# Bulk rows laid out by partition: one run of 126 rows per partition, stored without TensorE and PSUM

## Chip, cores, metric

One core of one Trainium2 chip. The metric is device time in microseconds (us) of one execution; the median of several executions is quoted, and a profiled execution gives the lines shown. A profile's span, from first to last instruction, is some 1.8 us shorter than the device time of the same run.

## The reference

```python
x = np.random.randn(64, 256, 8192).astype(np.float32)   # 536.87 MB
out = np.mean(x, axis=2)                                # 16,384 means, 64 KB
```

That is 16,384 rows of 8192 float32, 32 KiB each, read once.

## The kernel before

63 bulk loads bring 256 rows each (8 MiB) into one of three slots of SBUF: partition p gets two neighbouring rows, 64 KiB. VectorE sums both into `res`. The last 256 rows come in a cut-up tail, so that little is left to sum after the last byte. The results of the bulk lie with the row pair on partitions and the block number along the free axis; to store them in order, TensorE transposes `res`.

```python
NB = N // (P * R); LB = NB - 1                     # 64 blocks, 63 of them bulk; P = 128, R = 2
x_v = x_f.rearrange("(n p r) s -> n p r s", p=P, r=R)
out_bulk = o_f[0 : LB * P * R].rearrange("(n p r) -> n p r", p=P, r=R)
# ... (cut)
for n in range(LB):
    xt = slots[n % SLOTS]                          # SLOTS = 3
    ld = load(xt[:], x_v[n], load_sem[n % LOAD_SEMS])
    if n < LB - 1:
        loaded(n, dve_sum(res[:, :, n], xt[:]))
    else:                                          # last bulk block: half on ScalarE
        loaded(n, dve_sum(res[:, 0, n : n + 1], xt[:, 0, :]))
        loaded(n, act_sum(res[:, 1, n : n + 1], xt[:, 1, :]))
# ... (cut: the tail: head = 8192 columns of 128 rows, then 4096, 2048, ... 256, 256)
bulk = pool.tile([P, P, R], F32)
for r in range(R):
    ps = psum_pool.tile([P, P], F32, name=f"ps{r}")
    nc.tensor.transpose(out=ps[:LB, :], in_=res[:, r, :], identity=ident[:])
    nc.vector.tensor_scalar_mul(out=bulk[:LB, :, r], in0=ps[:LB, :], scalar1=inv)
nc.sync.dma_start(out=out_bulk, in_=bulk[:LB])     # 63 pieces of 1 KiB
# ... (cut: scaled sums and stores of the tail)
```

## Time and profile before

| | before |
|---|---|
| median of 3 runs | 1246.19 us (1246.14 to 1246.21) |
| span of the profiled run | 1244.9 us |
| VectorE busy | 1087.4 us, 87% |
| TensorE matmuls and weight loads | 0.9 + 0.4 us |
| DMA | 431 GB/s over the span |

### The profile page before, as it was taken

Reading aid. Unit: us, or ns where it says so; the run is one execution under the profiler, and the core shown is the slowest. Engines: PE = TensorE matmul, PEld = TensorE weight load, DVE = VectorE, ACT = ScalarE, POOL = GpSimd, SP = SyncE. Lnnn points to the kernel's source line nnn. Section 1 sums busy time; section 2 is a strip of 40 time slices with the busy share of each in tenths; the row PEclk is TensorE's granted clock in tenths of the full one; section 3 lists DMA queues with packets and bytes.
Section 4 is the critical chain, followed back from the end, with each engine's and each line's share of the span. In section 5 each row is a group of like instructions: output and inputs, shape, how many; then the busy total and the mean of one; then the engine's idle time right before and its main releaser. Section 6 shows DMA issues by size and latency. Waiting matters only on the chain.

```text
span 1244.9 us, 214 instructions
## 1 busy us (share of the span) xinstructions
PE 0.9 (0%) x2; PEld 0.4 (0%) x2; DVE 1087.4 (87%) x79; ACT 16.5 (1%) x13; POOL 0.7 (0%) x6
## 2 busy tenths in 40 slices
PE   0000000000000000000000000000000000000000
PEld 0000000000000000000000000000000000000000
DVE  3898988989889889898898988989889898898898
ACT  0000000000000000000000000000000000000004
POOL 0000000000000000000000000000000000000000
DMA  9999999999999999999999999999999999999998
GB/s 436 406 438 438 438 438 432 415 434 438 438 438 438 438 425 417 438 438 438 438 438 436 409 436 438 438 438 438 438 427 415 438 438 438 438 438 436 409 436 373
DMA packets 10169, 536.95 MB, mean 431 GB/s; under 512 B 1145, under 2 KB 1464, under 8 KB 1720
## 3 DMA queue, kind: packets, MB, share of 16 engines
q1 hardware_dynamic: 10168, 536.94, 99.8%
q14 instruction: 1, 0.01, 0.0%
HBM read 536.87 MB, written 0.07 MB: 431 GB/s over the span
## 4 chain that ended last, share of the span: by engine, by line
DMA 70%; DVE 29%; SPq 0%; issue 0%; DVEq 0%
DMA xt<-in_x_dram 70%; DVE res L92 29%; DVE fin_in L92 0%; SPq L82 0%; DVE fin_in L98 0%; DVE fin_t L109 0%; DVEq L98 0%
## 5 line engine op out<-in xcount | busy, mean ns | idle before, releaser
L92 DVE TENSOR_REDUCE res<-xt 128x2 f32<-128x16384 f32 (+1 forms) x63 | 1076.4, 17086 | 153.5 <-DMA xt<-in_x_dram 153.5
L95 ACT ACT_TABLE_LOAD x1 | 1.3, 1283 | 1181.5 <-DVE res L92 1181.5
L95 ACT ACTIVATE xt<-xt 128x8192 f32<-128x8192 f32 (+5 forms) x6 | 14.7, 2443 | 43.9 <-DMA xt<-in_x_dram 43.7
L92 DVE TENSOR_REDUCE fin_in<-xt 128x1 f32<-128x256 f32 (+3 forms) x5 | 5.0, 1004 | 0.3 <-DMA xt<-in_x_dram 0.2
L92 DVE TENSOR_REDUCE head<-xt 128x1 f32<-128x4096 f32 x1 | 4.4, 4420 | 0.2 <-DMA xt<-in_x_dram 0.2
L153 PE MATMUL ps<-ident,res 128*63 128x128 f32 x2 | 0.9, 458 | 1230.5 <-ACT xt L95 1229.5
L95 ACT ACTIVATION_READ_ACCUMULATOR xt<-xt 128x1 f32 x6 | 1.1, 186 | 0.0
L72 DVE MEMSET fin<- 128x32 f32 x2 | 0.1, 85 | 0.9 <-PEq L254 0.9
L154 DVE TENSOR_SCALAR bulk<-ps 63x128 f32<-63x128 f32 x2 | 0.6, 279 | 0.4 <-PE ps L153 0.4
L153 PEld LDWEIGHTS ps<-ident,res 128*63 128x63 f32 x2 | 0.4, 180 | 1230.8 <-issue 1229.4
L98 DVE TENSOR_SCALAR_CACHE_REDUCE fin_in<-fin_in 128x265 f32<-128x265 f32 x1 | 0.4, 431 | 0.2 <-DVE fin_in L92 0.2
L109 DVE STREAM_TRANSPOSE fin_t<-fin 128x32 f32<-128x32 f32 x2 | 0.4, 211 | 0.1
L60 POOL TENSOR_SCALAR_AFFINE_SELECT ident<-ident 128x128 f32<-128x128 f32 x1 | 0.3, 292 | 0.1
L98 DVE TENSOR_SCALAR_CACHE_REDUCE head<-head 128x2 f32<-128x2 f32 x1 | 0.2, 155 | 0.1
L59 POOL MEMSET ident<- 128x128 f32 x1 | 0.2, 204 | 0.4 <-POOLq L254 0.4
L254 POOL MEMSET const-bfloat16-1.0<- 128x1 bf16 x1 | 0.1, 101 | 0.0
L254 POOL MEMSET const-uint8-127<- 128x1 uint8 x1 | 0.1, 101 | 0.0
L254 POOL MEMSET const-float32-0.0<- 128x1 f32 x1 | 0.1, 98 | 0.2 <-issue 0.2
L254 POOL MEMSET const-float32-1.0<- 128x1 f32 x1 | 0.1, 98 | 0.0
L98 DVE DVE_READ_ACCUMULATOR head<-head 128x1 f32 x1 | 0.1, 83 | 0.0
L98 DVE DVE_READ_ACCUMULATOR fin_in<-fin_in 128x1 f32 x1 | 0.1, 83 | 0.0
## 6 DMA issues: line engine op xcount, KB each, us to landing
xt<-in_x_dram SPq DMA_DIRECT2D x1, 4096.0 KB, 31.1
xt<-in_x_dram SPq DMA_DIRECT2D x1, 2048.0 KB, 35.7
xt<-in_x_dram SPq DMA_DIRECT2D x1, 1024.0 KB, 37.7
xt<-in_x_dram SPq DMA_DIRECT2D x63, 40.8
xt<-in_x_dram SPq DMA_DIRECT2D x1, 512.0 KB, 38.5
xt<-in_x_dram SPq DMA_DIRECT2D x1, 256.0 KB, 38.7
xt<-in_x_dram SPq DMA_DIRECT2D x1, 128.0 KB, 38.6
fin_in<-in_x_dram SPq DMA_DIRECT2D x1, 128.0 KB, 38.4
```

The source lines that it names most:

```text
L59: nc.gpsimd.memset(ident[:], 0.0)
L60: nc.gpsimd.affine_select(out=ident[:], in_=ident[:], compare_op=mybir.AluOpType.not_equal, fill=1.0, base=0, pattern=[[-1, P]], channel_m ...
L72: nc.vector.memset(fin[r][:], 0.0)
L92: return untracked(nc.vector.tensor_reduce(out=dst, in_=src, axis=X, op=ADD))
L95: return untracked(nc.scalar.activation(out=src, in_=src, func=COPY, accum_out=dst))
L98: return nc.vector.tensor_scalar(out=src, in0=src, scalar1=inv, scalar2=None, op0=mybir.AluOpType.mult, op1=ADD, accum_out=dst,)
L109: nc.vector.transpose(out=fin_t[r][:], in_=fin[r][:])
L153: nc.tensor.transpose(out=ps[:LB, :], in_=res[:, r, :], identity=ident[:])
L154: nc.vector.tensor_scalar_mul(out=bulk[:LB, :, r], in0=ps[:LB, :], scalar1=inv)
L254: nc = _bacc.Bacc("TRN2", target_bir_lowering=False, num_devices=1)
```

## The change

Intent: let each partition own one run of 126 consecutive rows. Then its 126 sums are 126 consecutive results, 504 B, and go out straight from SBUF; identity, transposes, PSUM and the two evictions go.

```diff
-    x_v = x_f.rearrange("(n p r) s -> n p r s", p=P, r=R)
+    x_v = x_f[0 : LB * P * R].rearrange("(p n r) s -> n p r s", p=P, r=R)
-    out_bulk = o_f[0 : LB * P * R].rearrange("(n p r) -> n p r", p=P, r=R)
+    out_bulk = o_f[0 : LB * P * R].rearrange("(p n) -> p n", p=P)
     (cut: psum_pool and the identity go)
-    res = pool.tile([P, R, LB], F32)
+    res = pool.tile([P, LB * R], F32)
+    bulk = pool.tile([P, LB * R], F32)
-            loaded(n, dve_sum(res[:, :, n], xt[:]))
+            loaded(n, dve_sum(res[:, n * R : (n + 1) * R], xt[:]))
     (cut: the same for the last bulk block)
-    bulk = pool.tile([P, P, R], F32)
-    for r in range(R):
-        ps = psum_pool.tile([P, P], F32, name=f"ps{r}")
-        nc.tensor.transpose(out=ps[:LB, :], in_=res[:, r, :], identity=ident[:])
-        nc.vector.tensor_scalar_mul(out=bulk[:LB, :, r], in0=ps[:LB, :], scalar1=inv)
-    nc.sync.dma_start(out=out_bulk, in_=bulk[:LB])
+    nc.vector.tensor_scalar_mul(out=bulk[:], in0=res[:], scalar1=inv)
+    nc.sync.dma_start(out=out_bulk, in_=bulk[:])
```

In `x_v` the order of `n` and `p` is swapped: the pieces of one load, neighbours before, are now 126 rows = 4032 KiB apart.

More of the change, by code (lines that the diff above doesn't have):

```diff
@@ L37 @@
     LB = NB - 1
-    assert SLOTS <= LB <= P and sum(LAST_CHUNKS) == S
+    assert SLOTS <= LB and sum(LAST_CHUNKS) == S
     inv = 1.0 / float(S)
@@ L43 @@
     o_f = out.rearrange("b c -> (b c)")
-    x_v = x_f.rearrange("(n p r) s -> n p r s", p=P, r=R)
+    x_v = x_f[0 : LB * P * R].rearrange("(p n r) s -> n p r s", p=P, r=R)
     x_l = x_f[LB * P * R : N].rearrange("(r p) s -> r p s", p=P)
-    out_bulk = o_f[0 : LB * P * R].rearrange("(n p r) -> n p r", p=P, r=R)
+    out_bulk = o_f[0 : LB * P * R].rearrange("(p n) -> p n", p=P)
     out_last = o_f[LB * P * R : N].rearrange("(r q j) -> r q j", q=P // SQ, j=SQ)
     pool = ctx.enter_context(tc.tile_pool(name="sb", bufs=1))
-    psum_pool = ctx.enter_context(
-        tc.tile_pool(name="psum", bufs=1, space=bass.MemoryType.PSUM)
-    )
     slots = [nc.alloc_sbuf_tensor(f"xt{i}", [P, R, S], F32) for i in range(SLOTS)]
@@ L55 @@
     tail_sem = [tc.alloc_semaphore(f"tail{i}") for i in range(len(LAST_CHUNKS) + 1)]
-    res = pool.tile([P, R, LB], F32)
-    ident = pool.tile([P, P], F32)
-    nc.gpsimd.memset(ident[:], 0.0)
-    nc.gpsimd.affine_select(
-        out=ident[:],
-        in_=ident[:],
-        compare_op=mybir.AluOpType.not_equal,
-        fill=1.0,
-        base=0,
-        pattern=[[-1, P]],
-        channel_multiplier=1,
-    )
+    res = pool.tile([P, LB * R], F32)
+    bulk = pool.tile([P, LB * R], F32)
     fin = [pool.tile([P, SQ], F32, name=f"fin{r}") for r in range(R)]
@@ L117 @@
         if n < LB - 1:
-            loaded(n, dve_sum(res[:, :, n], xt[:]))
+            loaded(n, dve_sum(res[:, n * R : (n + 1) * R], xt[:]))
         else:
-            loaded(n, dve_sum(res[:, 0, n : n + 1], xt[:, 0, :]))
-            loaded(n, act_sum(res[:, 1, n : n + 1], xt[:, 1, :]))
+            loaded(n, dve_sum(res[:, n * R : n * R + 1], xt[:, 0, :]))
+            loaded(n, act_sum(res[:, n * R + 1 : n * R + 2], xt[:, 1, :]))
     nparts = 2 * len(LAST_CHUNKS)
```

## The prediction

> **What bounds the kernel now.** I read the page from the top: busy shares, the 40 slices, the chain that ended last, the costliest groups, then the timeline of the middle and of the last 30 us.
>
> ```profile
> PE 0.9 (0%) x2; PEld 0.4 (0%) x2; DVE 1087.4 (87%) x79; ACT 16.5 (1%) x13; POOL 0.7 (0%) x6
> ...
> DMA  9999999999999999999999999999999999999998
> GB/s 436 406 438 438 438 438 432 415 434 438 438 438 438 438 425 417 438 438 438 438 438 436 409 436 438 438 438 438 438 427 415 438 438 438 438 438 436 409 436 373
> ...
> DMA xt<-in_x_dram 70%; DVE res L92 29%; DVE fin_in L92 0%; SPq L82 0%; DVE fin_in L98 0%; DVE fin_t L109 0%; DVEq L98 0%
> ```
>
> The 16 DMA engines are full in every slice but the last. VectorE (DVE) has 29% of the chain, which looks like a second bound, so the next thing to read is whether it ever makes the DMA wait. The timeline of the middle says no:
>
> ```profile
> 602.98 17.22 DVE L92 TENSOR_REDUCE res<-xt 128x2 f32<-128x16384 f32 x1 [2.13 <-DMA xt<-in_x_dram]
> 622.34 17.22 DVE L92 TENSOR_REDUCE res<-xt 128x2 f32<-128x16384 f32 x1 [2.13 <-DMA xt<-in_x_dram]
> 641.69 17.22 DVE L92 TENSOR_REDUCE res<-xt 128x2 f32<-128x16384 f32 x1 [2.13 <-DMA xt<-in_x_dram]
> ```
>
> One reduction starts every 19.35 us, takes 17.22 us, and then stands 2.13 us until the next 8 MiB have landed. It frees its slot, and the load three further on is issued, while another whole load and the last 2.13 us of one are still queued, so the queue never runs dry. The chain passes through a reduction only because it follows the load's issue back to the freed slot. The cadence is a transfer rate: 8,388,608 B in 19.35 us is 433.5 GB/s. As 8 rows of 64 KiB per engine, a row takes 19.35 / 8 = 2.42 us, 27.1 GB/s per engine. Load time for all: 536.87 MB / 433.5 GB/s = 1238.5 us of the 1244.9 us span. The other 6.4 us are about 1 us before the first packet, some slower packets early on, and the last sum and store after the last load.
>
> What the change rewrites is all in the last 15 us:
>
> ```profile
> 1222.24 8.69 DVE L92 TENSOR_REDUCE res<-xt 128x1 f32<-128x8192 f32 x1 [2.13 <-DMA xt<-in_x_dram]
> 1229.18 0.19 ACT L95 ACTIVATION_READ_ACCUMULATOR xt<-xt 128x1 f32 x1
> 1229.43 0.18 PEld L153 LDWEIGHTS ps<-ident,res 128*63 128x63 f32 x1 [1229.43 <-issue]
> 1229.46 0.44 PE L153 MATMUL ps<-ident,res 128*63 128x128 f32 x1 [1229.46 <-ACT xt L95]
> 1230.85 0.27 DVE L154 TENSOR_SCALAR bulk<-ps 63x128 f32<-63x128 f32 x1
> 1230.98 0.18 PEld L153 LDWEIGHTS ps<-ident,res 128*63 128x63 f32 x1 [1.37 <-DVE res L92]
> 1230.98 0.47 PE L153 MATMUL ps<-ident,res 128*63 128x128 f32 x1 [1.08 <-DVE res L92]
> 1231.50 0.28 DVE L154 TENSOR_SCALAR bulk<-ps 63x128 f32<-63x128 f32 x1 [0.38 <-PE ps L153]
> 1231.81 0.37 SPq L155 DMA_DIRECT2D out_dram<-bulk  x1
> 1231.96 3.62 ACT L95 ACTIVATE xt<-xt 128x4096 f32<-128x4096 f32 x1 [2.59 <-DMA xt<-in_x_dram]
> 1231.96 4.42 DVE L92 TENSOR_REDUCE head<-xt 128x1 f32<-128x4096 f32 x1 [0.18 <-DMA xt<-in_x_dram]
> ```
>
> Transposes and evictions end at 1231.78; VectorE then idles 0.18 us until the next load (`head`) lands. That wait is what matters: the whole TensorE episode fits into a hole that a load closes.
>
> [...]
>
> **The change, part by part.**
>
> *Load addresses.* Still 63 loads of 128 rows of 64 KiB, the same count and piece size, into the same slots. What is new is the distance from one partition's piece to the next: before 64 KiB (one contiguous 8 MiB block), after 126 rows x 32 KiB = 4032 KiB, that is 4 MiB less 64 KiB. This is the only part that touches the 1238 us[...]. Working modulo a power of two: 4 MiB - 64 KiB = 63 x 64 KiB, and 63 is odd, so the 128 pieces of a load fall on 128 different 64 KiB places modulo 8 MiB, exactly as before, in a different order; modulo 4 MiB each partition steps 64 KiB backwards where it stepped 64 KiB forwards.[...] Cost: 0 us as my main case.
>
> *Removed work.* Two weight loads, two matmuls, two evictions from PSUM, and the two GpSimd instructions for the identity (0.20 + 0.29 us near the start, while the first load is under way). On VectorE, 0.27 + 0.28 us busy and a 0.38 us wait, 0.93 us in all, between 1230.85 and 1231.78. None lies on the path: 0 us.
>
> *Added work.* One multiply of 128x126 f32, SBUF to SBUF. Its size from two rows of one kind in this trace: the scaled sum takes 155 ns for 2 elements per partition and 431 ns for 265, so 1.05 ns per element over 153 ns. At that rate 126 elements take about 0.29 us (an estimate; without the accumulator perhaps less). It can start when the last bulk reduction ends (1222.24 + 8.69 = 1230.93; ScalarE was done at 1229.37) and ends at about 1231.2. VectorE's idle time before `head` grows from 0.18 to about 0.7 us and the store is issued about 0.55 us earlier. Both are slack: 0 us.
>
> *The store.* Before, 63 partitions of 1024 B; after, 128 of 504 B, 64,512 B in both. It is issued at 1231.8 on the queue where all loads have stood since 1204, and packets leave in order. The DMA view by windows shows it. Between 1231.8 and 1240.2:
>
> ```profile
> DMA packets 479, 3.42 MB, mean 407 GB/s; under 512 B 48, under 2 KB 48, under 8 KB 247
> ```
>
> There is no packet from 512 B to 2 KB here, so none of the 63 of the store; the next 1.3 us have 364 - 52 = 312 of the 319 (256 of the last two loads, 63 of the store), and the rest follow by 1241.64. So the store moves only behind the loads and issuing it earlier gains nothing. In the trace a 1024 B packet takes 46 ns and a 128 B packet of the last stores 11 to 13 ns[...]. Interpolating, 504 B is about 25 ns; with 8 pieces on each of 16 engines some 0.2 us per engine[...]. Even 0.2 us a piece would be 1.6 us from 1241.6 on, and the last store's packets leave at 1244.1. 0 us.
>
> *The end.* Last load, short reductions, scaled sum, transpose, store: the same instructions and sizes. The VectorE stream is shorter,[...] I give that +-0.3 us.
>
> Sum: 0 (loads) + 0 (TensorE, PSUM) + 0 (multiply) + 0 (store) +-0.3 us. 1246.19 stays 1246.2.
>
> **The rivals.** (a) *The far pitch slows the loads.* For it:[...] engines now read regions many MiB apart. Against: the 63-is-odd argument[...]. A full halving[...] would mean about 2,480 us; I give it 3%. A mild loss, one in which rows need 2.5 instead of 2.42 us, gives 3% or 1,280 us; 4%. A loss confined to the start would cost some us.
> (b) *The end shortens.* Less work before `head`, no TensorE, an earlier store. For it: 0.93 us of VectorE time shrinks to 0.3. Against: `head` starts on a load's landing in any case, and everything after follows landings. If wrong, about 1245.5, not 2%.
> (c) *The 504 B store becomes the last thing to finish.* If every piece cost about 0.5 us in series, 8 of them would end at about 1245.6 instead of 1241.6 and push the last store behind them; the time would be 1248. Against: the 128 B packets at 11 to 13 ns.
> (d) *Scheduling.* The multiply could be put among the last short reductions, which run back to back: about +0.3 us.
>
> **Range and chances.** Runs of before span 0.07 us. (b), (c) and (d) move at most 2 us; only (a) can leave the 2% (25 us), and only upwards. Predicted 1246.2 us, range 1244.8 to 1250 (small gains below, a mild or early loss or a slow store above). Faster by over 2%: 1%, since the loads alone take 1238.5 us[...]. Slower: 7%, from (a). Same: 92%.
>
> **What would show it.** Loads: the reductions still 19.35 us apart with 2.13 us idle, the slices still 438 GB/s; a longer cadence with more idle time before each reduction is (a). Removed work: no PE rows, one `bulk` multiply near 0.29 us, and `head` still starting at 1231.96 with 0.7 us of idle before it, put down to the DMA. Store: its packets of 504 B between 1240 and 1242, and the last packets still near 1244.1; anything later is (c). The prediction is wrong if the cadence leaves 19.3 to 19.5 us or if the time from the last landing to the end changes by more than 1 us.

## The result

| | before | after |
|---|---|---|
| median, runs side by side | 1246.20 us (4 runs) | 1246.18 us (1246.05 to 1246.46, 4 runs) |
| ratio after/before, 95% interval | | 1.000 (0.998 to 1.002): same |
| span of the profiled run | 1244.9 us | 1244.4 us |
| bulk cadence in the middle | 19.35 us | 19.35 us |

Ratios here and below are the mean time of one kernel's fast runs over that of the other's of the same rounds, so not quite the ratio of the medians quoted. The spans differ by 0.5 us, the unprofiled times by 0.02 us; I read nothing into the former.

The page of the kernel after, the lines that answer to those of the prediction:

```profile
DVE 1087.0 (87%) x78; ACT 16.5 (1%) x13; POOL 0.2 (0%) x4
...
DMA  9999999999999999999999999999999999999998
GB/s 432 423 426 438 438 438 438 436 430 415 438 438 438 438 438 432 417 432 438 438 438 438 432 417 432 438 438 438 438 436 419 426 438 438 438 438 436 426 419 373
DMA packets 10241, 536.95 MB, mean 431 GB/s; under 512 B 1280, under 2 KB 1536, under 8 KB 1792
```

PE and PEld are gone, and the DMA is as full as it was. Packets under 512 B rose from 1145 to 1280, by 135: the 128 pieces of the store, and 7 more packets of 4 B (1138 before, 1145 after, counted in the traces). The middle, from the timeline of the kernel after (start, duration, instruction, idle before and what ended it):

```profile
602.58 17.22 DVE L80 TENSOR_REDUCE res<-xt 128x2 f32<-128x16384 f32 x1 [2.13 <-DMA xt<-in_x_dram]
621.92 17.22 DVE L80 TENSOR_REDUCE res<-xt 128x2 f32<-128x16384 f32 x1 [2.13 <-DMA xt<-in_x_dram]
```

Here the new addresses show no effect at all. The end of the bulk, same view:

```profile
1221.80 8.69 DVE L80 TENSOR_REDUCE res<-xt 128x1 f32<-128x8192 f32 x1 [2.13 <-DMA xt<-in_x_dram]
...
1230.61 0.23 DVE L138 TENSOR_SCALAR bulk<-res 128x126 f32<-128x126 f32 x1
1230.86 0.35 SPq L139 DMA_DIRECT2D out_dram<-bulk  x1
...
1231.52 4.42 DVE L80 TENSOR_REDUCE head<-xt 128x1 f32<-128x4096 f32 x1 [0.68 <-DMA xt<-in_x_dram]
```

One multiply of 0.23 us stands where the 0.93 us of VectorE's waits and evictions stood. The time saved is in the brackets at the end: the idle time before `head` grew from 0.18 to 0.68 us, and a load still ends it. The distance from the start of the last bulk reduction to that of `head` is 9.72 us in both kernels (1231.96 - 1222.24; 1231.52 - 1221.80).

### The profile page after: what moved, and what is told of

It is laid out like the page before. It is cut to its first block, busy times and chain, and to the rows that moved or that the text cites. A ratio compares the mean times of both kernels' runs of the same rounds, so it can differ in the third digit from the quotient of the medians.

```text
span 1244.4 us, 203 instructions
## 1 busy us (share of the span) xinstructions
DVE 1087.0 (87%) x78; ACT 16.5 (1%) x13; POOL 0.2 (0%) x4
## 2 busy tenths in 40 slices
DMA packets 10241, 536.95 MB, mean 431 GB/s; under 512 B 1280, under 2 KB 1536, under 8 KB 1792
## 4 chain that ended last, share of the span: by engine, by line
DMA 70%; DVE 29%; SPq 0%; issue 0%; DVEq 0%
DMA xt<-in_x_dram 70%; DVE res L80 29%; DVE fin_in L80 0%; SPq L70 0%; DVE fin_in L86 0%; DVE fin_t L97 0%; DVEq L86 0%
## 5 line engine op out<-in xcount | busy, mean ns | idle before, releaser
L80 DVE TENSOR_REDUCE res<-xt 128x2 f32<-128x16384 f32 (+1 forms) x63 | 1076.3, 17085 | 153.1 <-DMA xt<-in_x_dram 153.1
## 6 DMA issues: line engine op xcount, KB each, us to landing
xt<-in_x_dram SPq DMA_DIRECT2D x1, 512.0 KB, 38.5
fin_in<-in_x_dram SPq DMA_DIRECT2D x1, 128.0 KB, 38.5
```

The costliest lines, as they stand in the source:

```text
L80: return untracked(nc.vector.tensor_reduce(out=dst, in_=src, axis=X, op=ADD))
```

## Experiments

Three questions: do two parts of the change cancel; is the end really slack, and how much; and what does the distance between the partitions' pieces cost, which the change takes from 64 to 4032 KiB. "Wrong" marks kernels whose sums are of other rows or go elsewhere; their instructions and sizes are those of the kernel named.

### Each half of the change alone

`loads_only` is the kernel before with the new addresses (wrong):

```diff
-    x_v = x_f.rearrange("(n p r) s -> n p r s", p=P, r=R)
+    x_v = x_f[0 : LB * P * R].rearrange("(p n r) s -> n p r s", p=P, r=R)
```

> Kernel before with the changed load addresses alone (4032 KiB between partitions); transposes, evictions and the 1 KiB store stay (wrong result on purpose, the sums go to other places). My theory, every part costs nothing by itself: 1246.2 us, reductions 19.35 us apart. Rival, two parts cancel: this one is off by some us one way and the next run by as much the other way.

`store_only` is the kernel after with that line turned back (wrong).

> Changed kernel with the loads of before (one contiguous 8 MiB block each; wrong result on purpose), so only TensorE's removal and the direct store of 504 B pieces. My theory: 1246.2 us, the first multiply ends some 0.7 us before the head load lands. Rival, cancellation: off from 1246.2 by as much as the run above, the other way.

Measured: `loads_only` 1246.26 us, ratio to before 0.9997 (0.9984 to 1.0011); `store_only` 1246.24 us, ratio 0.9998 (0.9984 to 1.0012); five runs each. Nothing cancels: each half is worth nothing within 0.2%. In `store_only` the idle time before `head` is again 0.68 us, in `loads_only` 0.17 us, so the shorter episode comes from the second half alone, as it should.

### How much slack the end has

`mul_21` repeats the multiply of the kernel after (right result):

```diff
-    nc.vector.tensor_scalar_mul(out=bulk[:], in0=res[:], scalar1=inv)
+    for _ in range(21):
+        nc.vector.tensor_scalar_mul(out=bulk[:], in0=res[:], scalar1=inv)
```

> Changed kernel with its multiply done 21 times, all ahead of the head reduction. 20 more at 0.228 us and about 0.03 us between them are 5.1 us. My theory: 0.68 us of idle before head and 0.2 us later on take up the first 0.9 us, the rest comes through, so about 4.2 us longer: 1250.4 us, with head started by the multiply and not by the DMA. Rival, VectorE's tail is not on the path at all: 1246.2 us. Rival, all of it is on the path: 1251.3 us.

Measured: 1249.34 us in the middle of five runs, 1249.32 to 1249.48; ratio 1.0022 (1.0009 to 1.0036). That is 3.2 us more than the kernel after, and 3.1 more than `store_only` of the same rounds, where 4.2 was expected. Timeline of `mul_21`:

```profile
1230.42 4.69 DVE L139 TENSOR_SCALAR bulk<-res 128x126 f32<-128x126 f32 x18
1231.32 3.62 ACT L83 ACTIVATE xt<-xt 128x4096 f32<-128x4096 f32 x1 [2.59 <-DMA xt<-in_x_dram]
...
1235.02 4.41 DVE L80 TENSOR_REDUCE head<-xt 128x1 f32<-128x4096 f32 x1
...
1240.07 4.65 DVE L80 TENSOR_REDUCE fin_in<-xt 128x1 f32<-128x2048 f32 x5
```

ScalarE starts on `head`'s other half as soon as it lands, at 1231.32; VectorE now comes 3.70 us later, and the wait for the DMA in its brackets is gone. The construction was not quite as planned: 18 of the 21 multiplies ran ahead of `head`, the other three between `head` and the next sums, where they lengthened the distance from the end of `head` to the first short sum from 0.47 to 0.64 us, by 0.17 us. And the short sums of the tail's later pieces, which VectorE writes to `fin_in` and of which every one now finds its data landed, take 4.80 us up to the scaled sum instead of 5.39 (1244.87 - 1240.07; 1241.80 - 1236.41): 0.59 us more of slack used up. 3.70 + 0.17 - 0.59 = 3.28 us, and from the landing of `head` to the end of the last transpose it is 14.24 us against 10.96, 3.28 us more. So the account closes: the VectorE work ahead of `head` is free up to the 0.68 us that it idles there, plus 0.59 us of later waits. The change moved within the first of these. My 4.2 us had the placing of three multiplies wrong and 0.2 us for the later waits instead of 0.59.

### What small pieces of the store cost

`store_4b` keeps the results two elements apart in SBUF, which cuts the store into 4 B pieces (right result):

```diff
-    bulk = pool.tile([P, LB * R], F32)
+    bulk = pool.tile([P, LB * R, 2], F32)
-    nc.vector.tensor_scalar_mul(out=bulk[:], in0=res[:], scalar1=inv)
-    nc.sync.dma_start(out=out_bulk, in_=bulk[:])
+    nc.vector.tensor_scalar_mul(out=bulk[:, :, 0], in0=res[:], scalar1=inv)
+    nc.sync.dma_start(out=out_bulk, in_=bulk[:, :, 0])
```

> Changed kernel with the results two elements apart in SBUF, so that the store goes out as 16,128 pieces of 4 B, 1008 on each engine (right result). My theory, a small piece costs some 9 to 12 ns and the store waits behind all loads: 9 to 12 us from 1240.4 us on instead of 0.8, so its end passes the last store's and the time is 1252 to 1255 us. Rival (c),[...] 0.2 us or more in series: 200 us or more on top, 1450 us.

Measured: 1328.65 us, ratio 1.066 (1.064 to 1.067). Both numbers were wrong: 82 us more, not 6 to 9 and not 200. The DMA view of `store_4b` between 1246 and 1300 us:

```profile
DMA packets 11289, 0.05 MB, mean 1 GB/s; under 512 B 11289, under 2 KB 11289, under 8 KB 11289
...
q1 hardware_dynamic: 11289, 0.05, 194.3%
```

11,289 packets in 54 us on 16 engines are 76.5 ns each, at 1 GB/s. The median packet of this store is recorded with 9 ns, but the median misleads: the last line gives these records 194.3% of 16 engines' time, so they overlap, and their mean is 149 ns (1.943 x 16 x 54 us / 11,289). The first ones went fast: by the records some 2,900 packets of 4 B, most of them pieces of the store, started between 1238 and 1242 us. So small writes to memory do have a price well above the median record; whether a first burst escapes it is the next question.

`store_56b` puts 14 results together, 1,152 pieces, fewer than that burst (right result):

```diff
-    bulk = pool.tile([P, LB * R], F32)
+    bulk = pool.tile([P, 9, 15], F32)
     (multiply and store use bulk[:, :, 0:14] and the result viewed as 9 x 14)
```

> Changed kernel with the results in SBUF in groups of 14 with a gap, so that the store goes out as 1,152 pieces of 56 B, 72 on each engine (right result). The 4 B store ran fast for its first 2,865 pieces and then at 74 ns per piece and engine. If the first pieces are taken in at their own speed: 72 x 11 ns = 0.8 us, hidden, 1246.2 us. If each small piece costs 74 ns from the first on: 5.3 us from 1240.4 us, about 2 us past the last store's issue, 1248 us.

Measured: 1247.62 us (1247.42 to 1248.09), ratio 1.0012 (0.9995 to 1.0029). Every run lies above every run of the kernel after, and of the kernel before in the same rounds (at most 1246.48); the interval of the ratio just includes 1. Timeline of `store_56b`:

```profile
1242.92 0.43 DVE L86 TENSOR_SCALAR_CACHE_REDUCE fin_in<-fin_in 128x265 f32<-128x265 f32 x1 [1.22 <-DMA fin_in<-in_x_dram]
```

and of the kernel after:

```profile
1241.80 0.43 DVE L86 TENSOR_SCALAR_CACHE_REDUCE fin_in<-fin_in 128x265 f32<-128x265 f32 x1 [0.15 <-DVE fin_in L80]
```

The last *load*, ahead of the store in the same queue, completes later: 39.8 us after its issue instead of 38.5. VectorE, which in the kernel after is held by its own last sum, now waits 1.22 us for it. Why small writes delay the completion of a load issued before them is left open.

The store itself also ends later. The DMA view of `store_56b`, with the wait of SyncE for the store at the very end of the program, and the DMA view of the kernel after, where SyncE has no such wait:

```profile
out_dram<-bulk SPq DMA_DIRECT2D x1, 63.0 KB, 14.1
SPq L219 <- DMA out_dram<-bulk: 0.9, 1, 0.9
...
out_dram<-bulk SPq DMA_DIRECT2D x1, 63.0 KB, 10.9
```

The pieces of 56 B all started by 1241.62, but the store, issued at 1231.0, landed 14.1 us later, near 1245.0; the one of the kernel after landed near 1241.8. From the first piece, at 1240.1, that is 4.9 us for 72 pieces on each engine, some 68 ns a piece on the slowest engine (an estimate from these times). That is close to the second of the two expectations, 74 ns from the first piece on and 1248 us: the burst was fast in its starts, not in its ends. Two delays are thus present, the load's and the store's, and the run does not separate their shares. With 504 B pieces the last load lands after 38.5 us, against 38.4 before, and the scaled sum does not wait for it.

### What the distance between the pieces costs

All variants are the kernel after with another distance from one partition's piece to the next. They read the same number of 64 KiB pieces and are wrong. The edit, for 4 MiB:

```diff
-    x_v = x_f[0 : LB * P * R].rearrange("(p n r) s -> n p r s", p=P, r=R)
+    x_v = x_f.rearrange("(p n r) s -> n p r s", p=P, r=R)
```

For the others with M rows between partitions, M below 126 (rows are then read more than once):

```diff
+    x_v = [
+        x_f[n * R : n * R + P * M].rearrange("(p m) s -> p m s", m=M)[:, 0:R, :]
+        for n in range(LB)
+    ]
```

> Changed kernel with the partitions exactly 128 rows = 4 MiB apart instead of 126 rows = 4032 KiB (wrong result on purpose: other rows are summed). Theory A (the odd 63 x 64 KiB is what saves the change[...]): the 128 pieces of a load fall on 2 places modulo 8 MiB, the reads go at about half rate or worse, rows of 64 KiB take about 5 us instead of 2.42, time about 2,480 us or more. Rival B ([...]the pitch of these 64 KiB reads does not matter at all): 2.42 us a row, 1246 us.

> The same with the partitions 64 rows = 2 MiB apart (wrong result on purpose, rows are read more than once). Theory A: 4 places modulo 8 MiB[...]. Rival B: 1246 us.

> The same with the partitions 16 rows = 512 KiB apart (wrong result on purpose, rows are read more than once). Theory A: 16 places modulo 8 MiB, as many as there are DMA engines, so little or no loss: 1246 to 1280 us. Rival B: 1246 us.

> The same with the partitions 112 rows = 3.5 MiB = 7 x 512 KiB apart (wrong result on purpose, rows are read more than once). Not a power of two, but even: 16 places modulo 8 MiB, as in the 512 KiB case. Theory A says that it behaves like the 512 KiB pitch (odd multiple of the same power of two), within 1%. A theory C, that only exact powers of two hurt, says 1246 us also where 512 KiB is slowed. Rival B: 1246 us for both.

Then the neighbourhood of 4 MiB, by `x` seen flat, with 1024, 128 or 8192 elements taken off the distance:

```diff
+    pitch = (4 << 20) // 4 - 1024        # less 4 KiB
+    x_p = x_f.rearrange("a s -> (a s)")[0 : P * pitch].rearrange("(p m) -> p m", m=pitch)
+    x_v = [x_p[:, n * R * S : (n + 1) * R * S].rearrange("p (r s) -> p r s", r=R) for n in range(LB)]
```

> Changed kernel with the partitions 4 MiB less 4 KiB apart (wrong result on purpose, rows are cut). The 4 MiB pitch took 1608 to 1745 us. Theory A as I stated it, places of 64 KiB modulo 8 MiB: 128 x 4 KiB span only 512 KiB, 8 of 128 places, so still clearly slow, 1400 us or more. Theory D,[...] 1246 us[...].

> The same, 4 MiB less 512 B (wrong result on purpose).[...] Theory A: as slow as the full 4 MiB, 1600 us or more. If offsets of any size are enough: 1246 us.

> The same, 4 MiB less 32 KiB, half of the offset that the change has (wrong result on purpose). Theory A: 64 places of 64 KiB, no loss, 1246 us. Theory D: 1246 us. If the change's 64 KiB were just barely enough: over 1260 us.

| distance | median us (runs) | ratio to before |
|---|---|---|
| 512 KiB | 1246.70 (1246.53 to 1246.81) | 1.0004 |
| 2 MiB | 1256.77 (1254.93 to 1257.30) | 1.0081 (1.0064 to 1.0098) |
| 3.5 MiB | 1246.47 (1246.42 to 1246.56) | 1.0002 |
| 4032 KiB (the change, in the rounds of the result) | 1246.18 (1246.05 to 1246.46) | 1.000 |
| 4 MiB - 32 KiB | 1246.21 (1246.13 to 1246.30) | 1.0000 |
| 4 MiB - 4 KiB | 1247.29 (1246.74 to 1247.86) | 1.0010 |
| 4 MiB - 512 B | 1251.97 (1251.01 to 1252.02) | 1.0046 (1.0029 to 1.0063) |
| 4 MiB | 1678.8 (1607.6 to 1744.65) | fastest run 1.29 |

The ratios are to the kernel before in the same rounds. The runs at 4 MiB scatter by over 8%, so three of the four count as slow by the rule that a run over 1.5% above the fastest of its kernel is slow; the profiled one is among them. No run is given a ratio with an interval, but the fastest is 361 us above any run of the kernel before, at a granted clock of 1.0 throughout. The page of `pitch_4m` (the slow, profiled run):

```profile
DVE 1087.0 (62%) x78; ACT 16.4 (1%) x13; POOL 0.2 (0%) x4
...
GB/s 275 302 302 299 292 305 293 289 292 310 299 302 296 308 308 293 302 305 302 299 298 310 293 307 295 316 313 302 316 298 320 332 305 329 335 320 343 346 361 306
```

and its timeline:

```profile
623.12 17.22 DVE L80 TENSOR_REDUCE res<-xt 128x2 f32<-128x16384 f32 x1 [9.97 <-DMA xt<-in_x_dram]
650.11 17.22 DVE L80 TENSOR_REDUCE res<-xt 128x2 f32<-128x16384 f32 x1 [9.78 <-DMA xt<-in_x_dram]
```

This is what rival (a) of the prediction looks like: the work on VectorE is the same to the tenth of a microsecond, and only the waits before it have grown, from 2.13 to some 10 us. Over the 63 bulk reductions VectorE waited 651.7 us for loads, against 153.1 in the kernel after: 498.6 us more, and the span is 498.4 us longer. GB/s over the span fell from 431 to 308 (this run is one of the slow ones; the fastest still took 1607.6 us). So the distance alone can slow the loads. Rival B, that the distance does not matter here, falls.

But theory A as I stated it falls too. It counted places of 64 KiB modulo 8 MiB: at 512 KiB and 3.5 MiB it allowed little or no loss, rightly, but at 2 MiB, with 4 places of 128 between the 2 at 4 MiB and the 16 at 512 KiB, a clear loss was to be expected, and it was 0.8%; 8 of 128 at 4 MiB less 4 KiB should have meant 1400 us and meant 1247. Theory D had 1246 us at 4 MiB less 4 KiB and less 32 KiB, and fits both times within 0.1%. Its argument was which addresses the engines read at the same moment; no run here shows which engine reads which piece, so the times bear out its numbers and not its cause. At 512 B less the loss is 0.5%. How much must be taken off 4 MiB is thus measured; why 4 MiB is bad is not shown. The timelines say where the small losses lie. `pitch_2m`:

```profile
26.24 17.22 DVE L83 TENSOR_REDUCE res<-xt 128x2 f32<-128x16384 f32 x1 [25.24 <-DMA xt<-in_x_dram]
48.14 17.22 DVE L83 TENSOR_REDUCE res<-xt 128x2 f32<-128x16384 f32 x1 [4.68 <-DMA xt<-in_x_dram]
69.29 17.22 DVE L83 TENSOR_REDUCE res<-xt 128x2 f32<-128x16384 f32 x1 [3.93 <-DMA xt<-in_x_dram]
88.89 17.22 DVE L83 TENSOR_REDUCE res<-xt 128x2 f32<-128x16384 f32 x1 [2.38 <-DMA xt<-in_x_dram]
108.91 17.22 DVE L83 TENSOR_REDUCE res<-xt 128x2 f32<-128x16384 f32 x1 [2.80 <-DMA xt<-in_x_dram]
128.23 17.22 DVE L83 TENSOR_REDUCE res<-xt 128x2 f32<-128x16384 f32 x1 [2.10 <-DMA xt<-in_x_dram]
```

The kernel after starts its first reduction at 22.07 us. Here it starts 4.2 us later, the next four waits exceed 2.13 us by 2.55, 1.80, 0.25 and 0.67 us, and from the sixth load on the waits are the usual ones: 9.4 of the 10.8 us by which the span is longer, lost in the first five loads. At 4 MiB less 512 B the first reduction starts at 24.89 us and only the second waits longer (3.43 us): 4.1 of 4.8 us. My reading is that the 16 engines start in step, hinder each other, and drift apart until they no longer do. The DMA view by windows can test the drifting. It books a packet's bytes where the packet starts; in a window of 20 us a slice is 0.5 us, so 16 pieces of 64 KiB, one per engine, add up to 2,097 GB/s. In this order: `pitch_2m` from 1 to 21 us and from 100 to 120 us, the kernel after from 100 to 120 us:

```profile
GB/s 918 524 655 0 0 0 0 262 1442 393 0 0 0 1180 655 262 0 0 393 1180 393 131 0 131 1049 786 131 0 0 262 918 655 262 0 0 786 786 262 131 131
GB/s 918 131 131 262 524 1049 262 0 262 524 262 786 262 131 655 262 786 262 131 655 524 655 131 393 393 918 393 0 393 524 786 393 131 393 524 786 262 131 655 262
GB/s 0 1311 786 0 0 0 1311 786 0 0 0 1835 262 0 0 131 1835 131 0 0 393 1573 131 0 0 918 1049 131 0 0 1311 786 0 0 0 1311 786 0 0 0
```

At 2 MiB the 16 pieces start together at first (918 + 524 + 655 is 2,097, then four empty slices), and by 100 us there is hardly an empty slice: the engines did drift apart, in the stretch in which the loss ends. In the kernel after they are still in step there, and it loses nothing (434 GB/s from 120 to 1200 us, as in the kernel before), so being in step does no harm by itself. That the drift is what ends the loss at 2 MiB is my reading; no run at 2 MiB keeps them in step. At exactly 4 MiB the loss doesn't end: the rate from 1000 to 1700 us is still 321 GB/s, after 300 from 100 to 1000 us.

None of these runs points to a version faster than the two kernels, and none was tried.

## Why the prediction was right

- **Bound by the rate of the loads.** Right: 19.35 us per load, 2.13 us of wait before each reduction, before and after.
- **Load addresses, 0 us.** Right in size, confirmed alone by `loads_only`. The reason held only in part. That the 64 KiB step keeps the change off a bad distance is shown: at 4 MiB the same kernel takes 1608 us or more. But the counting of 64 KiB places modulo 8 MiB was more than is needed; 32 KiB off is as good, and 4 KiB off costs about 1 us, which the interval (0.9993 to 1.0026) does not tell from nothing.
- **Removed work, 0 us.** Right: `store_only` alone does nothing, and the freed 0.5 us turned into idle time before `head`. From the start of `head` to the end of the last transpose it is 10.96 us instead of 10.98, well inside the 0.3 us allowed for the end.
- **The multiply, estimated at 0.29 us, starting and ending in the hole.** It took 0.23 us, less than the estimate, which was made from an instruction with an accumulator; the prediction had allowed for that. The idle time was given as about 0.7 us and was 0.68.
- **The store, 0 us.** Right for the 504 B pieces, and part of the argument was weak. I took the 11 to 13 ns records of the 128 B packets as proof that small writes are cheap. `store_4b` shows a price of 76.5 ns per piece where the median record says 9 ns, and `store_56b` that a store can land 3.4 us after its last piece has started and that small writes can also delay the end of the last load. That the estimate held was partly luck: 128 pieces are few. In the kernel after they took 27 ns (median) and started by 1241.2 us, close to the 25 ns interpolated, and the last store's packets left at 1243.7, about 0.4 us earlier with the whole tail.
- **Rivals.** (b), the end shortens, did not happen. (c), the store ends last, did not happen: the store landed near 1241.8, ahead of the last store's packets at 1243.7, and the 0.5 us per piece that (c) needs is far above the 76.5 ns of `store_4b`. (d), a multiply among the last sums, did not happen: it ran right behind the last bulk reduction. (a) was rightly kept as the only way out of the 2%, but its size was off: even at the worst distance tried the time is 1608 to 1745 us, not 2,480; the profiled run kept 308 GB/s over its span. Its mild case was also summed short: rows of 2.5 us make 1,280 us for the loads alone, 1,286 with the other 6.4 us.

## What to carry to other kernels

An engine at 87% and a chain that runs through it for 29% can still have no say: read what ends its idle time, and follow a saving to the next wait before counting it. When a layout change alters only the distance between the partitions' pieces, the transfer count, the piece size and even the DMA's busy digits can look the same (all 9 but the last slice at 4 MiB too) and the time can still be decided by it: read the GB/s line. For reads like these, in pieces of 64 KiB, 32 KiB less than 4 MiB was far enough; other multiples of 4 MiB were not tried. Here the natural round number, 128 rows per partition, would have cost 29% or more, and 126 rows cost nothing.
